# Encoder block on one core: order of the opening, products without use in front, low weights on GpSimd

## The chip, the cores and the metric

The kernel runs on one core of one Trainium2 chip, as one program. The metric is the device time of an execution in microseconds (us). Before the change it is 1885.11 us, the median of 3 runs (1883.92 to 1886.2).

## The reference, cut to what matters

One layer is applied to two groups of tokens, 2048 and 512 of them (five windows of 512), each with 16 meta tokens, at a width of 1024.

```python
u = rms_norm(h, norm_g)                    # h * rsqrt(mean(h*h) + eps) * g
qa, ka, va, za, qb, kb, vb, zb, ga, gb = jnp.split(u @ w_in, cuts, axis=-1)
o_a = neighbourhood_attention(qa, ka, va, na_rpb, n)
o_b = window_attention(qb, kb, vb, t5_bias, sink, n)
merged = sigmoid(ga) * ((o_a * silu(za)) @ w_proj_a) + sigmoid(gb) * ((o_b * silu(zb)) @ w_proj_b)
h = h + merged @ w_out                     # then a final rms_norm
```

Only the first part matters here: the norm and the projection of the last window (window 4) by 18 blocks of `w_in`, each 128 columns wide, and the passage to the next stage, which projects windows 0 and 1 together.

## The kernel before

**Split operands.** Every float32 operand of a product is kept as two tiles, a high one (the value rounded, made by ScalarE) and a low one (value minus high, made by VectorE or GpSimd). A product is three matmuls: high weight by high data (L146), high by low (L147), low weight by high data (L148). `split_part` (L206 to 208) does this for weights: L207 is the cast on ScalarE, L208 the subtraction on the engine that is passed in, else on VectorE in this stage. `split_w` (L210) does a weight block in two halves of 512 columns, so each block is two casts and two subtractions.

**The opening.** `start_w` fetches the first weight blocks, `prep_last` (L317) loads window 4 in four tiles `xt` of two row blocks each. For each row block `k` it makes the high operand on ScalarE (L334, a scaling by the norm's gain) and the low one on VectorE (L335). Then ScalarE squares the tile in place (L337) and VectorE adds the squares to `rs` (L339, L342). The row scale by the root of the mean square isn't applied to the operands but to the results, at eviction, so projections can start before the roots are known. After a first `yield`, `prep_last` sums `rs` over partitions with small matmuls (L360, L361), computes the roots on VectorE (`rsqrt`, L150 to 163, on five columns) and puts them on the diagonal of a tile (L177). After a second `yield` it spreads them over all partitions with matmuls (`spread`, L185) and copies them to `rs` (L370).

**The first stage.** `beside` (L933) runs the 18 projections one after the other. `alone` does one of them: it yields four times in a projection, and `beside` counts these yields in `q`. At `q` = 9 and `q` = 14 (the pair `own[1]`) it resumes `prep_last`. Until the second of these points the evictions are held back in a list (`held[1]`), since they need the roots; there it runs them. Before projection `i` the weights of projection `i + 1` are split and those of projection `i + 3` fetched. Weight buffers are double, so the cast of a block waits for the end of the projection before the last. `prep_first`, resumed at the counts in `at`, prepares windows 0 and 1 for the next stage in the meantime: squares (L418) and sums of squares (L420, L423: one window on VectorE, the other on GpSimd), roots, scalings (L377) and operand splits (L381 on ScalarE, L382 on VectorE). Its tiles of squares and the `xt` share one pool of four buffers (`ev`). Projections 0 to 7 make queries; 8 to 17 make keys and values, each in two parts of 256 and 272 columns.

**The passage.** After the last projection `sides_first` makes sums of weight blocks (L816 to L829) and splits them, and `begin` and `pairs` start the paired stage, whose products are all recorded at L850 (`product`).

**What sets the order.** TensorE's and SP's instructions stand in the order of the code. Those of ScalarE, VectorE and GpSimd are put in order by a scheduler when the program is built, from times that it assumes; on the chip each engine works its queue strictly in that order. Every DMA shown below is issued by SP through `move` (L142).

Of the kernel before, what the change touches and what calls it, by code (L numbers as in the profile page):

```python
# [9 lines left out]
F32 = mybir.dt.float32  # L10
F32R = mybir.dt.float32r
I32 = mybir.dt.int32
AF = mybir.ActivationFunctionType
# [4 lines left out]
P = 128  # L18
# [7 lines left out]
WTOK = 512  # L26
# [69 lines left out]
def encoder_block(ctx: ExitStack, tc: tile.TileContext, xT, x_end, w_in, w_pa, w_pb, w_o, norm_g, final_g,  # L96
                  final_row, bias_a0, bias_a1, bias_a2, bias_a3, bias_b, bias_b0, outT_p, outT_s, out_e):
    nc = tc.nc
# [29 lines left out]
    ones_r = const.tile([P, P], F32R, name="ones")  # L128
# [81 lines left out]
    def split_w(raw, engines=()):  # L210

        wt = wpool.tile([P, 2, KT * P], F32R, tag="wt", name="wt")
        for i, c in enumerate(range(0, KT * P, 4 * P)):
            split_part(wt[:, 0, c : c + 4 * P], wt[:, 1, c : c + 4 * P], raw[:, c : c + 4 * P], *engines[i : i + 1])
        return wt
# [94 lines left out]
    ps_t = ph.enter_context(tc.tile_pool(name="ps_t", bufs=3, space=PSUM))  # L310
# [6 lines left out]
    def prep_last(meta):  # L317


        w = NWIN - 1  # L320
        uh, ul = (operand(i, [P, KT, PITCH], f"u4{i}") for i in (5, 6))
        us[w] = (uh, ul, us[w][2] if w in us else uxp.tile([P, UW + N_META], F32, tag="rs4", name="rs4")[:, :UW])
        rs = us[w][2]
        for k in range(0, KT, 2):
            rows = xT[k * P : (k + 2) * P]
            xt = ev.tile([P, 2, WTOK], F32, tag="ev", name="xt")
            move(xt, rows[:, w * WTOK : (w + 1) * WTOK].rearrange("(k p) t -> p k t", p=P))
            if meta and k == 0:
                xm = st.tile([P, KT, N_META], F32, tag="xm", name="xm", bufs=1)
                move(xm, xT[:, TOK:].rearrange("(k p) t -> p k t", p=P))  # L330
            for j in range(2):
                g = ng[:, k + j : k + j + 1]
                h = uh[:, k + j, :WTOK]
                nc.scalar.mul(h, xt[:, j, :], g)  # L334
                nc.vector.scalar_tensor_tensor(ul[:, k + j, :WTOK], xt[:, j, :], g, f32(h), ALU.mult, ALU.subtract)  # L335
            if meta:
                nc.scalar.activation(xt, xt, AF.Square)  # L337
                if k == 0:
                    nc.vector.tensor_add(rs[:, :WTOK], xt[:, 0, :], xt[:, 1, :])  # L339
                else:  # L340
                    for j in range(2):
                        nc.vector.tensor_add(rs[:, :WTOK], rs[:, :WTOK], xt[:, j, :])  # L342
        if not meta:
            return
        t = ev.tile([P, WTOK], F32, tag="t", name="xms", bufs=3)
        a, b = (t[:, i * P : (i + 1) * P].rearrange("p (k m) -> p k m", m=N_META) for i in range(2))
        nc.vector.tensor_mul(a, xm, ng[:, :, None].broadcast_to([P, KT, N_META]))
        mh, ml = uh[:, :, WTOK:UW], ul[:, :, WTOK:UW]
        nc.scalar.copy(mh, a)
        nc.vector.tensor_sub(ml, a, f32(mh))  # L350
        nc.scalar.activation(b, xm, AF.Square)
        for n in (4, 2):
            nc.vector.tensor_add(b[:, :n], b[:, :n], b[:, n : 2 * n])
        nc.vector.tensor_add(rs[:, WTOK:], b[:, 0], b[:, 1])
        yield
        sq = st.tile([P, 32], F32, tag="sq", name="sq", bufs=1)[:, :5]
        nc.vector.memset(sq, 1.0)
        v = ps_t.tile([P, WTOK], F32, tag="vt", name="fin_v")
        for c in range(4):
            nc.tensor.matmul(v[:, c : c + 1], rs[:, c * P : (c + 1) * P], ones[:, 0:1], start=True, stop=True)  # L360
        nc.tensor.matmul(v[:N_META, 4:5], rs[:, WTOK:], ones[:, 0:1], start=True, stop=True)  # L361
        nc.scalar.copy(sq[:, :4], v[:, :4])
        nc.scalar.copy(sq[:N_META, 4:5], v[:N_META, 4:5])
        r = rsqrt(uxp, sq, P, 5)
        dgs = [ev.tile([P, WTOK], F32, tag="t", name="rs_dg", bufs=3) for _ in range(2)]
        diagonal(dgs[0], r[:, :4], P)
        diagonal(dgs[1], r[:N_META, 4:5], N_META)
        yield
        for dg, c0, m, nc_ in (dgs[0], 0, P, 4), (dgs[1], WTOK, N_META, 1):
            nc.scalar.copy(rs[:, c0 : c0 + nc_ * m], spread(ps_t, "vt", dg, m, nc_)[:, : nc_ * m])  # L370
        yield
# [561 lines left out]
    def beside(fs, raws, wts, own, wa, steps, at, zeros=iter(())):  # L933

        held = [own, None if own is None else []]
        ws = [*fs, *both[0]]
        lag[0] = 4
        mark[0] = None  # L940
        at = list(at)
        q = 0
        for i, f in enumerate(fs):
            if i:
                wts.append(split_w(raws[i + 1]))
                if i + 3 < len(ws):
                    raws.append(fetch_w(w_in[ws[i + 3]]))
                next(zeros, None)
            for _ in alone(f, wts[i], held):
                q += 1  # L950
                if own is not None and q in own[1]:
                    next(own[0])
                    if q == own[1][-1]:
                        for fn in held[1]:
                            fn()
                        held[1] = None
                while at and at[0] <= q:
                    at.pop(0)
                    next(steps)
                tick()  # L960
        for r in steps:
            if r == "last":
                break
        first = sides_first(raws[-2:], wts[-1])
        raw1 = fetch_w(w_in[both[1][0]])
        a = begin(both[0][0], wa, wts[-1], us[wa], ev)
        with tc.issue_after(copied[0]):
            for _ in steps:
                pass
        return a, first, raw1  # L970
# [8 lines left out]
    def start_w(fs):  # L979
        raws = [fetch_w(w_in[f]) for f in fs[:1]]  # L980
        wts = [split_w(raws[0])]
        yield raws, wts
        raws.append(fetch_w(w_in[fs[1]]))
        raws.append(fetch_w(w_in[fs[2]]))
        yield
        wts.append(split_w(raws[1]))
        raws.append(fetch_w(w_in[fs[3]]))
        yield

    def pass_(wa, a, first, raw1, ahead, extra, opening):  # L990
        with ExitStack() as pp:
            pool = [pp.enter_context(tc.tile_pool(name=f"p{i}", bufs=1, reuse_waits="tile")) for i in range(3)]
            return pairs(pool, wa, wa + 1, both, a, first.send(pool[2]), raw1, ahead, extra, opening)

    w0 = start_w(firsts)
    raws, wts = next(w0)
    own = prep_last(True)
    next(own)
    with tc.tile_pool(name="sp", bufs=1, reuse_waits="tile") as sp:
        loaded = []  # L1000
        steps = prep_first(sp, 0, loaded)
        next(w0)
        next(steps)
        next(w0)
        loaded.append(last_move[0])
        next(steps)
        zeros = zero_rows()
        next(zeros)
        begun = beside(firsts, raws, wts, (own, (9, 14)), 0, steps, [2, 20, 27, *(28 + 27 * i // 10 for i in range(16))],
                       zeros)  # L1010
    steps = [(0, 1), *((n, i) for n in range(1, KT) for i in (0, 1)), (KT, 0), (KT, 1), (KT, 2), (9, 1),
             *((j, i) for j in range(10, 18) for i in ((0, 2) if j % 2 == 0 else (1,)))]
# [680 lines left out]
```

## Time and profile before

| | before |
|---|---|
| median of 3 runs | 1885.11 us |
| the profiled execution | 1884.6 us |
| its span | 1882.6 us |
| TensorE (PE) busy | 1857.5 us, 99% |
| VectorE (DVE) busy | 1326.1 us, 70% |
| ScalarE (ACT) busy | 1144.5 us, 61% |
| GpSimd (POOL) busy | 729.2 us, 39% |
| TensorE's first product | 7.12 us |
| TensorE's first product of the paired stage | 122.38 us |

Times are in us from the start of the span. PE stands for TensorE, DVE for VectorE, ACT for ScalarE, POOL for GpSimd, SP for the engine that issues the DMAs. A row of a timeline gives the start, the time, the engine, the line of the code, the operation, what it writes and reads with shapes, and how many such instructions it merges; in brackets stands how long the engine had been idle, and what ended that. The time of a row covers an instruction's whole pipeline, so rows that follow each other overlap a little; from start to start a VectorE operation on 128 x 512 takes about 0.6 us where its row shows 0.68.

### The profile page before, as it was taken

The page shows a single profiled execution, that of the slowest core. Times are in us where ns is not written, and L with a number is a line of the kernel's source. Part 1 is how long each engine was busy: PE and PEld are TensorE (multiplying, and loading weights), DVE is VectorE, ACT ScalarE, POOL GpSimd, SP SyncE. Part 2 cuts the span into 40 slices and gives each one's busy share as a digit, 9 for nine tenths or more (in the row PEclk, how much of TensorE's full clock was granted, in tenths as well). Part 3 has the DMA queues.
Part 4 walks back from the last instruction along what each step waited for, and adds up shares of the span by engine and source line. Part 5 has one row for each costly group of instructions (what it writes and reads, how often), then busy time and mean ns, then how long its engine had stood idle before and what let it go on. Part 6 is the DMA issues. An engine that isn't in the chain of part 4 may idle for free. (4 is left out here: it accounts for less than half of the span.)

```text
span 1882.6 us, 29816 instructions
## 1 busy us (share of the span) xinstructions
PE 1857.5 (99%) x9797; PEld 1585.1 (84%) x9797; DVE 1326.1 (70%) x2961; ACT 1144.5 (61%) x2528; POOL 729.2 (39%) x558
## 2 busy tenths in 40 slices
PE   8999999999999999999999999999999999999998
PEld 6988888888888888888888888888888888888887
DVE  8985667556477565544457888878887877888874
ACT  6444444434365444444456797797789778878932
POOL 2005343323203222322324435656744763685420
PEclk9999999999999999999999999999999999999999
DMA  7675666655295677644259878977986997697483
GB/s 262 199 195 183 194 184 182 209 188 179 84 341 185 189 216 199 208 139 160 104 187 316 274 221 265 305 213 249 319 275 187 316 307 227 218 315 259 118 301 133
DMA packets 288145, 414.35 MB, mean 220 GB/s; under 512 B 117736, under 2 KB 162360, under 8 KB 286456
## 3 DMA queue, kind: packets, MB, share of 16 engines
q1 hardware_dynamic: 287704, 412.45, 68.1%
q8 instruction: 78, 1.28, 0.3%
q14 instruction: 75, 0.61, 0.1%
q10 hardware_dynamic: 288, 0.01, 0.0%
HBM read 303.46 MB, written 108.91 MB: 219 GB/s over the span
## 5 line engine op out<-in xcount | busy, mean ns | idle before, releaser
L208 POOL TENSOR_TENSOR wt<-wraw,wt 128x512 fp32r<-128x512 f32 x164 | 213.0, 1317 | 266.9 <-ACT wt L207 266.8
L850 PE MATMUL pa<-u,wt 128*128 128x512 f32 x1008 | 244.5, 392 | 2.1 <-ACT wt L207 1.1
L850 PE MATMUL pa<-u,x 128*128 128x512 f32 x984 | 236.7, 389 | 0.4 <-ACT u L861 0.4
L850 PEld LDWEIGHTS pa<-u,wt 128*128 128x128 f32 x1008 | 189.9, 189 | 42.4 <-ACT wt L207 1.5
L207 ACT CAST wt<-wraw 128x512 fp32r<-128x512 f32 x312 | 178.0, 619 | 74.8 <-PE mm L148 29.8
L850 PEld LDWEIGHTS pa<-u,x 128*128 128x128 f32 x984 | 184.5, 188 | 39.2 <-ACT u L861 0.8
L821 POOL TENSOR_TENSOR s<-wraw,raw 128x512 f32<-128x512 f32 x40 | 58.2, 1456 | 279.4 <-DVE x L208 279.4
L146 PE MATMUL mm<-u,wt 128*128 128x512 f32 (+2 forms) x416 | 150.4, 362 | 7.1 <-ACT u L334 7.1
L816 POOL TENSOR_TENSOR s<-raw 128x512 f32<-128x512 f32 x40 | 58.1, 1454 | 232.8 <-DMA raw<-in_w_in_dram 116.0
L147 PE MATMUL mm<-u,wt 128*128 128x512 f32 (+2 forms) x416 | 146.8, 353 | 1.1 <-DVE u L335 1.1
L148 PE MATMUL mm<-u,wt 128*128 128x512 f32 (+2 forms) x416 | 146.6, 352 | 0.0
L208 DVE TENSOR_TENSOR wt<-wraw,wt 128x512 fp32r<-128x512 f32 x148 | 104.5, 744 | 52.3 <-ACT wt L207 52.1
L850 PE MATMUL pe<-u,wt 128*128 128x512 f32 x504 | 121.4, 390 | 0.0
L850 PE MATMUL pc<-u,wt 128*128 128x512 f32 x504 | 121.1, 389 | 0.0
L850 PE MATMUL pe<-u,x 128*128 128x512 f32 x480 | 115.3, 389 | 0.0
L850 PEld LDWEIGHTS pe<-u,wt 128*128 128x128 f32 x504 | 94.6, 188 | 19.6
L850 PEld LDWEIGHTS pc<-u,wt 128*128 128x128 f32 x504 | 94.6, 188 | 19.6
L1145 DVE TENSOR_TENSOR pl<-tp,ph 128x384 fp32r<-128x384 f32 (+6 forms) x160 | 94.9, 593 | 20.9 <-ACT ph L1144 18.7
L1144 ACT CAST ph<-tp 128x384 fp32r<-128x384 f32 (+6 forms) x160 | 81.5, 510 | 43.0 <-PE tp L1141 41.4
L146 PE MATMUL pso<-mh,wt 128*128 128x512 f32 x256 | 107.1, 418 | 0.0
L829 POOL TENSOR_TENSOR s<-wraw,s 128x512 f32<-128x512 f32 x40 | 54.0, 1350 | 136.3 <-DVE wt L208 136.3
L850 PEld LDWEIGHTS pe<-u,x 128*128 128x128 f32 x480 | 90.1, 188 | 18.7
(258 smaller groups left out, 5024.8 us busy)
## 6 DMA issues: line engine op xcount, KB each, us to landing
wraw<-in_w_in_dram SPq DMA_DIRECT2D x86, 512.0 KB
raw<-in_w_in_dram SPq DMA_DIRECT2D x40, 512.0 KB
q<-qa SPq DMA_DIRECT2D x40, 512.0 KB
wraw<-in_w_o_dram SPq DMA_DIRECT2D x32, 512.0 KB
kbt<-kb SPq DMA_DIRECT2D x32, 384.0 KB
qa<-evq SPq DMA_DIRECT2D x20, 512.0 KB
qb<-evq SPq DMA_DIRECT2D x20, 512.0 KB
ka<-evk SPq DMA_DIRECT2D x20, 512.0 KB
```

Source lines behind the costliest of these rows:

```text
L146: nc.tensor.matmul(ps, wh, uh, start=first, stop=False)
L147: nc.tensor.matmul(ps, wh, ul, start=False, stop=False)
L148: nc.tensor.matmul(ps, wl, uh, start=False, stop=last)
L207: nc.scalar.copy(h, r)
L208: low[0] = (eng or lo_eng[0]).tensor_sub(l, r, f32(h)).ins
L816: eng.tensor_add(s1, a21, a22)
L821: eng.tensor_sub(s3, a11, a21)
L829: eng.tensor_sub(s4, a12, s2)
L850: nc.tensor.matmul(ps, wt[:, a, s], u[:, b, kk, :], start=first and kk == 0 and i == 0, stop=kk == 3 and i == 2, skip_group_check=True)
L1144: nc.scalar.copy(ph_[:kb, a], tb)
L1145: nc.vector.tensor_sub(pl_[:kb, a], tb, f32(ph_[:kb, a]))
```

## The change

Four things are changed.

1. In `prep_last` the squares come after all scalings in the code. Their sums are made by two engines: GpSimd adds the squares of the first two tiles, VectorE those of the last two, and VectorE adds the two sums.
2. Ahead of everything TensorE multiplies a tile of ones by itself 22 times, into a bank that nobody reads.
3. In `beside`, for the 18 projections of window 4, low weights go to GpSimd: the second half of the blocks split at `i` = 2 and 3, both halves from `i` = 4 on.
4. `prep_last` is resumed for the spread at `q` = 16 instead of 14, the end of the fourth projection instead of its middle.

Nothing else is edited, but the scheduler puts ScalarE's, VectorE's and GpSimd's instructions into another order up to about 140 us.

```diff
+        xts = []
         for k in range(0, KT, 2):
...
-            if meta:
-                nc.scalar.activation(xt, xt, AF.Square)
-                if k == 0:
-                    nc.vector.tensor_add(rs[:, :WTOK], xt[:, 0, :], xt[:, 1, :])
-                else:
-                    for j in range(2):
-                        nc.vector.tensor_add(rs[:, :WTOK], rs[:, :WTOK], xt[:, j, :])
+            xts.append(xt)
         if not meta:
             return
+        for xt in xts:
+            nc.scalar.activation(xt, xt, AF.Square)
+        parts = xts[0][:, 0, :], rs[:, :WTOK]
+        for sums_, first, eng in (parts[0], xts[0][:, 0, :], nc.gpsimd), (parts[1], xts[2][:, 0, :], nc.vector):
+            n = 0 if eng is nc.gpsimd else 2
+            eng.tensor_add(sums_, first, xts[n][:, 1, :])
+            for j in range(2):
+                eng.tensor_add(sums_, sums_, xts[n + 1][:, j, :])
+        nc.vector.tensor_add(parts[1], parts[1], parts[0])
...
-                wts.append(split_w(raws[i + 1]))
+                wts.append(split_w(raws[i + 1], (nc.vector if i < 4 else nc.gpsimd, nc.gpsimd) if own is not None and i > 1
+                                   else ()))
...
+    idle = ps_t.tile([P, WTOK], F32, tag="vt", name="idle")
+    for _ in range(22):
+        nc.tensor.matmul(idle[:, :P], ones_r, ones_r, start=True, stop=True)
...
-        begun = beside(firsts, raws, wts, (own, (9, 14)), 0, steps, [2, 20, 27, *(28 + 27 * i // 10 for i in range(16))],
+        begun = beside(firsts, raws, wts, (own, (9, 16)), 0, steps, [2, 20, 27, *(28 + 27 * i // 10 for i in range(16))],
```

On VectorE in the opening, from the third low operand on (`u` is the operand of window 4, `rs` its sum of squares, `wt<-wraw` a low weight), the rows before are:

```order
L335 SCALAR_TENSOR_TENSOR u_293<-xt,ng,u_292 128x512
L354 TENSOR_TENSOR rs_294<-xms 128x16
L335 SCALAR_TENSOR_TENSOR u_293<-xt,ng,u_292 128x512
L339 TENSOR_TENSOR rs_294<-xt 128x512
L335 SCALAR_TENSOR_TENSOR u_293<-xt,ng,u_292 128x512 x2
L342 TENSOR_TENSOR rs_294<-rs_294,xt 128x512
L335 SCALAR_TENSOR_TENSOR u_293<-xt,ng,u_292 128x512
L342 TENSOR_TENSOR rs_294<-rs_294,xt 128x512
L335 SCALAR_TENSOR_TENSOR u_293<-xt,ng,u_292 128x512
```

and now (lines below the edit are numbered 1 to 8 higher):

```order
L336 SCALAR_TENSOR_TENSOR u_316<-xt,ng,u_315 128x512
L358 TENSOR_TENSOR rs_317<-xms 128x16
L336 SCALAR_TENSOR_TENSOR u_316<-xt,ng,u_315 128x512 x5
L208 TENSOR_TENSOR wt<-wraw,wt 128x512 x2
L345 TENSOR_TENSOR rs_317<-xt 128x512
```

The three adds between the low operands are gone; GpSimd has three adds of `xt` in front of its queue instead. ScalarE's queue of the opening is the same in both programs, squares of the first two tiles between the scalings.

On GpSimd, after those three adds, the sums of squares of `prep_first` (`rsp`) were followed by the paired stage's first sum of weights:

```order
L420 TENSOR_TENSOR rsp_349<-sq 128x512
L423 TENSOR_TENSOR rsp_349<-rsp_349,sq 128x512 x6
```

and now the low weights stand between and behind them:

```order
L424 TENSOR_TENSOR rsp_372<-sq 128x512
L427 TENSOR_TENSOR rsp_372<-rsp_372,sq 128x512 x2
L208 TENSOR_TENSOR wt<-wraw,wt 128x512
L427 TENSOR_TENSOR rsp_372<-rsp_372,sq 128x512 x4
L208 TENSOR_TENSOR wt<-wraw,wt 128x512 x29
```

Thirty halves of low weights have moved to GpSimd's queue; VectorE's has lost as many.

On ScalarE at the passage to the paired stage (`wt<-s` are casts of sums of weights, `s<-pa` a copy of a bank, `u<-x` parts of the last operands) stood:

```order
L207 CAST wt<-s 128x512
L861 COPY s_1640<-pa 128x512
L381 CAST u_1661<-x_352 128x512 x4
L381 CAST u_1670<-x_353 128x512
L207 CAST wt<-s 128x512
L381 CAST u_1670<-x_353 128x512 x3
```

and now:

```order
L207 CAST wt<-s 128x512 x2
L865 COPY s_1663<-pa 128x512
L385 CAST u_1684<-x_375 128x512 x4
L385 CAST u_1693<-x_376 128x512 x4
```

The second cast of a weight sum has moved ahead of the copy and of all operand parts. On VectorE the two low halves of these sums have likewise moved ahead of all of them (the second stood behind five), and the first of the sums ahead of the last projection's last eviction.

## The prediction

> **What bounds the kernel now.** I read the page first, then the windows of 20 us, then TensorE's waits and the timelines of single engines.
>
> ```profile
> span 1882.6 us, 29816 instructions
> PE 1857.5 (99%) x9797; PEld 1585.1 (84%) x9797; DVE 1326.1 (70%) x2961; ACT 1144.5 (61%) x2528; POOL 729.2 (39%) x558
> ```
>
> TensorE is busy for 99%, so only its holes can be won, or new ones made. The program's rows differ from those of before only up to about 140 us, so these windows matter:
>
> ```profile
> 0.00:20.00 20.00, 12.59 (x43) 9.40 (x44) 14.84 (x30) 16.00 (x24) 1.97 (x7) 1.00 0.93 329
> 20.00:40.00 20.00, 18.98 (x93) 15.62 (x92) 19.04 (x32) 11.32 (x18) 8.47 (x7) 1.00 0.57 202
> 120.00:140.00 20.00, 17.93 (x83) 14.40 (x82) 15.07 (x29) 10.32 (x20) 1.18 (x1) 0.91 0.77 234
> ```
>
> After the window's length come the busy times of PE, PEld, DVE, ACT and POOL, the granted clock and DMA. Holes are before 20 us, one between 20 and 40, and one after 120, with the clock at 0.91. TensorE's waits up to 150 us, and its timeline, name them:
>
> ```profile
> PE pa L850 <- ACT wt L207: 1.1, 1, 1.1
> PE rs_rb L185 <- DVE rs_dg L177: 1.0, 1, 1.0
> PE pa L850 <- DVE wt L208: 1.0, 1, 1.0
> ...
> 7.12 0.79 PE L146 MATMUL mm<-u,wt 128*128 128x512 f32 x1 [7.12 <-ACT u L334]
> 11.89 0.39 PE L147 MATMUL mm<-u,wt 128*128 128x512 f32 x1
> 15.21 0.50 PE L147 MATMUL mm<-u,wt 128*128 128x512 f32 x1 [0.30 <-DVE u L335]
> 15.78 0.39 PE L146 MATMUL mm<-u,wt 128*128 128x512 f32 x1
> 31.72 1.48 PE L185 MATMUL rs_rb<-rs_dg,ones 128*128 128x128 f32 x10 [1.02 <-DVE rs_dg L177]
> ```
>
> A product takes 0.79 us at first and 0.39 from 11.89; the first projection ends at 15.78, its last piece late because VectorE's low half of it was late.
>
> **Idle products: 0.** They raise the clock before 7.12. That would be worth some 2.5 us (ten products in the 4.8 us from 7.12 to 11.89, against 0.23 each at full clock, twelve in 2.76 in the rows of the transition below) if operands were there. They are not: TensorE had caught up by 15.21 and waited. The first projection's end is set by VectorE, next.
>
> **Squares added by two engines: +1.4.** VectorE and ScalarE in the opening:
>
> ```profile
> 10.35 0.69 DVE L339 TENSOR_TENSOR rs<-xt 128x512 f32<-128x512 f32 x1
> 10.96 1.42 DVE L335 SCALAR_TENSOR_TENSOR u<-xt,ng,u 128x512 fp32r<-128x512 f32 x2
> 12.53 0.69 DVE L342 TENSOR_TENSOR rs<-rs,xt 128x512 f32<-128x512 f32 x1
> 13.14 0.75 DVE L335 SCALAR_TENSOR_TENSOR u<-xt,ng,u 128x512 fp32r<-128x512 f32 x1
> 13.81 0.68 DVE L342 TENSOR_TENSOR rs<-rs,xt 128x512 f32<-128x512 f32 x1
> 14.41 0.74 DVE L335 SCALAR_TENSOR_TENSOR u<-xt,ng,u 128x512 fp32r<-128x512 f32 x1
> ...
> 9.28 1.04 ACT L337 ACTIVATE xt<-xt 128x1024 f32<-128x1024 f32 x1
> 10.23 1.32 ACT L334 ACTIVATE u<-xt,ng 128x512 fp32r<-128x512 f32 x2
> 11.45 1.04 ACT L337 ACTIVATE xt<-xt 128x1024 f32<-128x1024 f32 x1
> 12.40 1.32 ACT L334 ACTIVATE u<-xt,ng 128x512 fp32r<-128x512 f32 x2
> ```
>
> ScalarE's queue keeps its order: two squares still stand ahead of the last two pairs of scalings, so the eighth low half can't start before about 13.8 (12.40 + 1.32, and the seventh's 0.75 from 13.14). Without the add at 13.81 it would run at 13.8 instead of 14.41: a gain of 0.6 to 0.7, if GpSimd's three adds cost nothing. What they cost VectorE is seen where both engines run:
>
> ```profile
> 25.69 5.43 POOL L423 TENSOR_TENSOR rsp<-rsp,sq 128x512 f32<-128x512 f32 x4 [2.26 <-ACT sq L418]
> ...
> 27.04 0.17 DVE L162 TENSOR_TENSOR rs<-rs,rs 128x5 f32<-128x5 f32 x1
> 27.24 1.15 DVE L163 SCALAR_TENSOR_TENSOR rs<-rs,rs 128x5 f32<-128x5 f32 x1
> ...
> 141.43 1.75 POOL L821 TENSOR_TENSOR s<-wraw,raw 128x512 f32<-128x512 f32 x1
> ...
> 141.95 0.68 DVE L281 TENSOR_TENSOR tq<-pe,u 128x512 f32<-128x512 f32 x1
> ```
>
> An operation on five columns, normally 0.17, takes 1.15 beside GpSimd's adds (1.36 each). One that reads PSUM passes in its usual 0.68. So a GpSimd add holds up a VectorE operation with two SBUF inputs for 1.15, and when both queues are full they alternate. The Trainium skill says the same, and it speaks against this change (SBUF — State Buffer, "Who interferes with whom"): a VectorE instruction with two SBUF inputs contends with a GpSimd one that reads SBUF, and the second to issue waits for the whole of the first. The trace agrees, 1.15 against 0.17.
>
> Applied to the opening: the first add starts at 10.4 (after the square from 9.28) and ends its hold at 11.6; low halves five and six run to 13.0; the second add holds to 14.15; the seventh runs to 14.8; the third add holds to 15.95; the eighth ends at 16.6. The first projection then ends at 17.15 instead of 15.78: +1.4, with -0.7 as the other end.
>
> **Roots spread later: -1.0.** The spread moves from half of the fourth projection to its end, 12 products or 2.7 us later. The roots come some 1.5 to 2 us later (the sums start 1.4 later, and one low weight is put ahead of them), so the wait of 1.02 goes; all of it returns if they are over 3.7 us late (2.7 + 1.02). Evictions start later with it, and so do stores on SP and the weight fetch queued behind them (L142); that is in the next term.
>
> **GpSimd makes low weights: +1.6.** The stretch from 51 to 122.5 us by engine, then L281 and L208 alone:
>
> ```profile
> 51.00:122.50 71.50, 71.50 (x556) 69.91 (x555) 66.23 (x131) 34.26 (x68) 0.00 (x0) 1.00 0.62 182
> ...
> 51.00:122.50 71.50, 10.65 (x23) 1.00 0.62 182
> ...
> 51.00:122.50 71.50, 15.59 (x24) 0.00 (x0) 1.00 0.62 182
> ```
>
> VectorE loses 24 low weights, 14.4 us at 0.6 from start to start, and keeps 51.8. GpSimd gains 24 that hold it up for 1.15 each: 27.6. GpSimd is then busy for about 24 x 1.3 = 31 of 71.5 us (44%), so that share of L281's 10.65, which reads PSUM, passes beside it: 4.6. Sum: 51.8 + 27.6 - 4.6 = 74.8 in 71.5. VectorE ends 3.3 us late. Of this TensorE feels between nothing (operands of the next stage are done early) and all (ScalarE's casts stand in one queue behind values that VectorE makes); I take the middle, 1.6. Where it shows first:
>
> ```profile
> 59.05 0.62 ACT L207 CAST wt<-wraw 128x512 fp32r<-128x512 f32 x1 [3.26 <-DMA wraw<-in_w_in_dram]
> 61.43 0.28 PE L146 MATMUL mm<-u,wt 128*128 128x256 f32 x1
> ```
>
> This cast ends 1.8 us ahead of its projection, and a low half now takes 1.3 instead of 0.6. A fetch 1 us later already stalls, and this one will be late: it stands in SP's queue (L142) behind the stores of the first evictions, which now start after the later spread. SP waits longer there too: a fetch into a buffer needs the low half that read it, now GpSimd's, some 2 us after the cast instead of 1.2. Behind such a fetch stand only stores of q, k and v, which nobody reads in this stretch, and the next fetch, two projections (some 11 us) ahead of its use. The evictions are held back half a projection longer, with four of five PSUM banks in use; the fifth projection takes the fifth, so TensorE doesn't wait for that.
>
> **Transition: -4.2.** The first products of the paired stage:
>
> ```profile
> 122.38 2.92 PE L850 MATMUL pa<-u,wt 128*128 128x512 f32 x12
> 125.14 2.88 PE L850 MATMUL pc<-u,wt 128*128 128x512 f32 x12
> 129.09 0.73 PE L850 MATMUL pa<-u,wt 128*128 128x512 f32 x2 [1.07 <-ACT wt L207]
> 130.82 4.14 PE L850 MATMUL pa<-u,wt 128*128 128x512 f32 x10 [1.00 <-DVE wt L208]
> 134.81 2.91 PE L850 MATMUL pe<-u,wt 128*128 128x512 f32 x12
> ...
> 128.42 0.62 ACT L207 CAST wt<-s 128x512 fp32r<-128x512 f32 x1
> ...
> 130.09 0.68 DVE L208 TENSOR_TENSOR wt<-s,wt 128x512 fp32r<-128x512 f32 x1
> ```
>
> Twelve take 2.76, so pe should start at 122.38 + 3 x 2.76 = 130.66; it starts at 134.81, 4.15 late: two waits and then products at 0.4 each. ScalarE cast the operand at 128.42, behind five others, and VectorE made its low half at 130.09. In the new order both casts stand ahead of those five and both low halves ahead of all operand parts. VectorE needs some 3.2 us from the last eviction to the first of them (three sums, evictions, one low half), so even 3 us late it has it near 129 against 127.9. I take -4.2; the other end is 0, if VectorE comes over 4 us late and the clock falls again.
>
> **Sum.** 0 + 1.4 - 1.0 + 1.6 - 4.2 = -2.2 us. The profiled run took 1884.6 (span 1882.6), 0.5 under the median of 1885.11. Median forecast: 1882.9.
>
> **Rivals.** *Nothing is lost to contention*: VectorE's late work has slack everywhere, operand low halves slip past GpSimd's adds: -0.7 - 1.0 + 0 - 4.2 = -5.9, 1879.2. For it: operands of the next stage are finished early. Against: the 1.15 rows. 0.27.
>
> *VectorE and GpSimd together become the bound* (slower): no PSUM read lies beside a GpSimd operation and TensorE feels all: 51.8 + 27.6 - 71.5 = +7.9, held at weight after weight from 61 us on. 1.4 - 1.0 + 7.9 - 4.2 = +4.1, 1889.2. It ends slower by over 0.2% once this term passes 7.6. For it: the stretch has only 5.3 us of VectorE idle. 0.18.
>
> *The clock falls in the opening* (a cost on top of the forecast): at full clock the first projection waits about 1.1 us three times, and the rows at 129.09 and 130.82 show two such waits followed by ten products in 4.14. That adds some 1.8: -0.4, 1884.7. The Trainium skill (TensorE: Matmul & The Clock Gate, "What's actually happening") has the clock fall only after an idle window of about 3.4 us; by that nothing is added. The trace shows the fall after waits of 1.07 and 1.00 with two products between, so I keep a chance: 0.13.
>
> **How the numbers follow.** The forecast has 0.42. Runs of this kernel can tell about 0.2% (3.8 us: 1881.3 to 1888.9) from no change. An eighth of the forecast's chance lies below 1881.3: faster 0.27 + 0.05 = 0.32; slower 0.18; the same 0.37 + 0.13 = 0.50. The range takes in the first rival nearly whole and reaches to the second: 1878.5 to 1889.2.
>
> **What would show it.** Idle products right: full clock at 7 us, first projection's end unmoved by them. Adds right: VectorE's fifth to eighth low halves 1 us and more each. Roots right: no wait at L185. Low weights right: GpSimd operations at 1.3 to 1.75, VectorE near full from 51 us, waits at L146 or L148 for GpSimd's weights. Transition right: both casts before 125 us and no wait at L850. Wrong is the forecast if the first projection ends before 15.5, if TensorE stalls over 4 us between 55 and 122, or if the waits at L850 stay.

## The result, and the profile after

The change makes the kernel slower: 1895.01 us (median of 6 runs, 1892.29 to 1897.69) against 1884.64 for the kernel before (6 runs), a ratio of 1.0052 with a 95% interval of 1.0039 to 1.0065. The profiled execution took 1892.8 us, 8.2 more than the one of before.

The profile's first lines, then the windows of 20 us and the stretch of the low weights, as for before:

```profile
span 1891.0 us, 29886 instructions
PE 1864.6 (99%) x9819; PEld 1588.7 (84%) x9819; DVE 1329.7 (70%) x2928; ACT 1144.2 (61%) x2528; POOL 780.3 (41%) x591
```

```profile
20.00:40.00 20.00, 20.00 (x98) 16.33 (x97) 19.38 (x25) 10.51 (x17) 15.97 (x11) 1.00 0.64 219
60.00:80.00 20.00, 18.03 (x134) 16.85 (x134) 19.07 (x26) 8.49 (x16) 9.33 (x6) 1.00 0.54 187
80.00:100.00 20.00, 18.08 (x143) 17.46 (x143) 19.96 (x31) 8.73 (x18) 10.95 (x6) 1.00 0.52 168
120.00:140.00 20.00, 16.95 (x108) 14.77 (x107) 16.15 (x29) 9.54 (x21) 6.73 (x4) 1.00 0.69 178
51.00:131.00 80.00, 74.47 (x560) 70.84 (x559) 69.86 (x107) 34.36 (x67) 38.25 (x24) 1.00 0.54 162
```

The hole between 20 and 40 us is gone. New ones of 2 us each stand in 60 to 80 and 80 to 100. The last row is the stretch of before's row from 51 to 122.5, now 80 us long because the paired stage starts at 130.87 instead of 122.38. TensorE's waits up to 170 us (total, times, longest) name the new holes:

```profile
PE mm L148 <- POOL wt L208: 3.0, 2, 1.9
PE vt L642 <- DVE vn L254: 1.6, 1, 1.6
PE idle L1002 <- DVE ones L129: 1.6, 1, 1.6
PE pa L854 <- ACT s L865: 1.1, 1, 1.1
PE mm L146 <- ACT wt L207: 0.9, 1, 0.9
...
PE pa L854 <- DVE wt L208: 0.3, 1, 0.3
```

How far the changed kernel is behind, from the starts of the same projections in the two timelines:

| | before | after | behind |
|---|---|---|---|
| second projection | 15.78 | 17.09 | 1.31 |
| fifth | 36.00 | 36.01 | 0.01 |
| ninth | 61.43 | 63.37 | 1.94 |
| tenth | 67.31 | 70.95 | 3.64 |
| thirteenth | 84.93 | 90.74 | 5.81 |
| seventeenth | 109.99 | 116.65 | 6.66 |
| paired stage | 122.38 | 130.87 | 8.49 |
| its product pe | 134.81 | 141.02 | 6.21 |

At the fifth projection the changed kernel has made good what it lost in the opening; all that follows is new. Most steps up are a wait or two. The first and the second of the large ones in four queues (SP's fetch, ScalarE's cast, GpSimd's low halves, TensorE's products):

```profile
58.03 0.32 SPq L142 DMA_DIRECT2D qb<-evq  x1
58.45 0.38 SPq L142 DMA_DIRECT2D wraw<-in_w_in_dram  x1
```

```profile
62.70 1.14 ACT L207 CAST wt<-wraw 128x512 fp32r<-128x512 f32 x2 [2.23 <-DMA wraw<-in_w_in_dram]
80.63 0.62 ACT L385 CAST u<-tt 128x512 fp32r<-128x512 f32 x1 [1.96 <-DVE tt L449]
81.16 1.13 ACT L207 CAST wt<-wraw 128x512 fp32r<-128x512 f32 x2
```

```profile
63.39 3.21 POOL L208 TENSOR_TENSOR wt<-wraw,wt 128x512 fp32r<-128x512 f32 x2 [5.94 <-ACT wt L207]
81.85 4.33 POOL L208 TENSOR_TENSOR wt<-wraw,wt 128x512 fp32r<-128x512 f32 x2 [4.87 <-ACT wt L207]
```

```profile
63.37 0.38 PE L146 MATMUL mm<-u,wt 128*128 128x256 f32 x1 [0.88 <-ACT wt L207]
64.96 0.38 PE L148 MATMUL mm<-u,wt 128*128 128x256 f32 x1 [1.09 <-POOL wt L208]
85.00 0.39 PE L148 MATMUL mm<-u,wt 128*128 128x256 f32 x1 [1.90 <-POOL wt L208]
```

The fetch left SP 4.2 us later than before (54.23), behind a store of values that VectorE made late. So the cast came 3.65 us later than before's 59.05, and two halves that had taken VectorE 0.69 us each took GpSimd 3.21. At 81 us no fetch is late: ScalarE's cast stands in its queue behind a value that VectorE made late (`tt`, a wait of 1.96), and the two low halves take 4.33.

Groups of GpSimd and of VectorE from 51 to 131 us (count, busy time, mean ns of one):

```profile
L208 POOL TENSOR_TENSOR wt<-wraw,wt 128x512 fp32r<-128x512 f32 x24 | 38.2, 1615 | 43.9 <-ACT wt L207 43.9
```

```profile
L386 DVE TENSOR_TENSOR u<-x,u 128x512 fp32r<-128x512 f32 x12 | 14.8, 1229 | 0.0
L281 DVE TENSOR_TENSOR tkv<-mm,rs 128x256 f32<-128x256 f32 x18 | 7.2, 407 | 0.0
L465 DVE TENSOR_TENSOR x<-x,tt 128x512 f32<-128x512 f32 x4 | 6.7, 1681 | 0.1
```

The first of VectorE's lines as it was before, from 51 to 122.5 us:

```profile
L382 DVE TENSOR_TENSOR u<-x,u 128x512 fp32r<-128x512 f32 x12 | 8.0, 682 | 0.0
```

Low halves of operands, 682 ns before, take 1229; L281, which reads PSUM, is as short as before (416 then).

### The profile page after: what moved, and what is told of

The parts are those of the page before. It is cut to its first block, busy times and chain, and to the rows that moved or that the text cites. A ratio compares the mean times of both kernels' runs of the same rounds, so it can differ in the third digit from the quotient of the medians.

```text
span 1891.0 us, 29886 instructions
## 1 busy us (share of the span) xinstructions
PE 1864.6 (99%) x9819; PEld 1588.7 (84%) x9819; DVE 1329.7 (70%) x2928; ACT 1144.2 (61%) x2528; POOL 780.3 (41%) x591
## 4 chain that ended last, share of the span: by engine, by line
PE 80%; DVE 6%; DMA 6%; ACT 4%; issue 2%; SPq 1%; POOL 1%; ACTq 0%; DVEq 0%
PE pa L854 23%; PE pe L854 11%; PE pc L854 6%; PE tp L1149 3%; PE mm L147 2%; PE mm L148 2%; PE mm L146 2%; PE pso L148 2%; PE pso L146 2%; PE pso L147 2%; DMA sgb<-gb 2%; PE psa L146 2%; PE psa L148 2%; PE psa L147 2%; PE tp L1251 2%
## 5 line engine op out<-in xcount | busy, mean ns | idle before, releaser
L208 POOL TENSOR_TENSOR wt<-wraw,wt 128x512 fp32r<-128x512 f32 x194 | 260.0, 1358 | 317.7 <-ACT wt L207 317.5
L207 ACT CAST wt<-wraw 128x512 fp32r<-128x512 f32 x312 | 177.8, 619 | 55.0 <-DMA wraw<-in_w_in_dram 19.2
L208 DVE TENSOR_TENSOR wt<-wraw,wt 128x512 fp32r<-128x512 f32 x118 | 87.3, 777 | 47.2 <-ACT wt L207 47.0
L1062 ACT ACTIVATE s<-s,nm 128x384 f32<-128x384 f32 (+5 forms) x160 | 87.1, 544 | 30.9 <-DVE nm L1055 29.9
```

The costliest lines, as they stand in the source:

```text
L207: nc.scalar.copy(h, r)
L208: low[0] = (eng or lo_eng[0]).tensor_sub(l, r, f32(h)).ins
L1062: nc.scalar.activation(out, s, AF.Exp, bias=nm, scale=-1.0, accum_out=sm)
```

## Experiments

Twelve more programs ran, one of them the kernel before itself. Each ratio is against the kernel before, run beside it. "Paired stage" is its first product in the profile, "pe" the product that started 12.43 us behind it before.

| run | ratio | 95% interval | paired stage | to pe |
|---|---|---|---|---|
| before | | | 122.38 | 12.43 |
| before, profiled again | | | 123.72 | 12.26 |
| after | 1.0052 | 1.0039 to 1.0065 | 130.87 | 10.15 |
| e1_low_on_vector | 1.0017 | 1.0008 to 1.0027 | 123.36 | 13.63 |
| e2_low_alone | 1.0049 | 1.0031 to 1.0067 | 130.73 | 10.36 |
| e3_unused_adds | 1.0071 | 1.0055 to 1.0086 | 134.67 | 12.84 |
| e4_one_half | 1.0007 | 0.9997 to 1.0017 | 125.88 | 9.18 |
| e5_idle_alone | 1.0003 | 0.9992 to 1.0014 | 122.15 | 12.41 |
| e6_squares_alone | 1.0022 | 1.0014 to 1.0031 | 123.81 | 14.08 |
| e7_spread_alone | 1.0004 | 0.9996 to 1.0013 | 121.42 | 12.30 |
| e8_late_halves | 0.9981 | 0.9972 to 0.9989 | 121.93 | 9.52 |
| e10_wide_idle | 1.0006 | 0.9997 to 1.0015 | 122.98 | 10.87 |
| e11_two_halves | 0.9981 | 0.9972 to 0.9990 | 121.55 | 8.19 |
| e12_unused_zeros | 1.0009 | 0.9999 to 1.0019 | 124.82 | 10.85 |

### The changed kernel with low weights on VectorE again

```diff
-                wts.append(split_w(raws[i + 1], (nc.vector if i < 4 else nc.gpsimd, nc.gpsimd) if own is not None and i > 1
-                                   else ()))
+                wts.append(split_w(raws[i + 1]))
```

> The changed kernel with all low weights of the first stage back on VectorE; squares, idle products and the later spread stay. Three theories. Port: GpSimd's subtractions hold up VectorE by some 1.15 us each, VectorE comes late, and weights and casts behind it: then the loss goes, about 1885 us (1883 to 1887), no waits for weights from 55 to 122 us. Late weight: a low weight takes 1.3 us on GpSimd instead of 0.6 and delays the fetch behind it, and VectorE's being held has no part in it: 1885 us too. Late spread: the evictions moved to the end of the fourth projection make stores and fetches late, GpSimd is not the cause: 1892 us or more, with the waits at 62 to 85 us still there.

Measured: 1888.75 us, and the paired stage at 123.36, 7.5 us earlier than in the changed kernel. TensorE's waits at the passage:

```profile
PE pa L854 <- ACT wt L207: 2.1, 1, 2.1
...
PE pa L854 <- DVE wt L208: 1.2, 1, 1.2
```

So the loss up to 131 us hangs on GpSimd's low weights, and the better passage too: without them the scheduler puts the second cast behind the copy and seven operand parts again. SP's late fetch leaves at 56.92 here, and no wait over 0.2 us follows: of the 4.2 us by which it is late in the changed kernel, 2.7 come from the other three parts and are covered by slack, and 1.5 come from GpSimd's low weights. The other three parts together still cost 0.08% to 0.27%.

### The kernel before with GpSimd's low weights alone

```diff
-                wts.append(split_w(raws[i + 1]))
+                wts.append(split_w(raws[i + 1], (nc.vector if i < 4 else nc.gpsimd, nc.gpsimd) if own is not None and i > 1
+                                   else ()))
```

> The kernel before with low weights on GpSimd as the only change. Port and late weight: 1889 to 1895 us, waits for GpSimd's low weights between 60 and 125 us. Late spread: 1881 to 1885 us, since the evictions stand where they did.

Measured: 1894.38, a loss as large as the changed kernel's from this part alone; the paired stage starts at 130.73 with the spread where it was. So the loss doesn't need the later spread. It is made up otherwise, though: 3.0 us stand ahead of the fifth projection (38.98 against 36.00), where TensorE waits 2.4 us for the roots and the granted clock is then 0.87 from 36 to 44 us. Later come a wait of 1.9 for a low weight and one of 1.1 for `vn`, as at 85 and 125 us in the changed kernel; the two waits at 63 us don't occur, so these need the change's other parts as well.

### Subtractions on GpSimd that nobody waits for

VectorE keeps every low weight. GpSimd subtracts 384 columns twice per block into columns that nobody reads.

```diff
                 wts.append(split_w(raws[i + 1]))
+                for n in range(0 if own is None or i < 2 else 2):
+                    h = f32(wts[-1][:, 0, n * 4 * P : n * 4 * P + 384]).rearrange("p (k c) -> p k c", k=KT)
+                    nc.gpsimd.tensor_sub(us[NWIN - 1][n % 2][:, :, UW:PITCH], h, h)
```

> The kernel before, with two subtractions on GpSimd beside each weight block from the third on (128 x 384, read from the block's high half, written to columns that nobody reads), 32 in all; VectorE still makes every low weight, and no fetch or product waits for GpSimd. Port: VectorE has 66.2 us of work between 51 and 122.5 us and is held up for 24 x 0.9 = 21.6 more, less some 3 beside PSUM reads: 85 in 71.5 us, so 8 to 14 us slower, 1893 to 1899 us. Late weight: no weight comes from GpSimd, so 1884 to 1886 us. Late spread: the same 1884 to 1886 us.

Measured: 1898.34, more than the change itself. TensorE now waits for VectorE's low weights, and VectorE is all but full:

```profile
PE mm L148 <- DVE wt L208: 3.9, 4, 2.1
PE rs_rb L185 <- DVE rs_dg L177: 3.3, 1, 3.3
PE pa L850 <- DVE wt L208: 1.6, 1, 1.6
```

```profile
51.00:134.50 83.50, 79.64 (x578) 75.86 (x577) 79.04 (x143) 35.15 (x68) 29.11 (x24) 0.98 0.56 168
```

Nobody waits for these subtractions, so what GpSimd holds up on VectorE is enough for a loss of this size; 5.5 of the 12.3 us stand ahead of the fifth projection (41.48 against 36.00), where the roots come late. That GpSimd's slow delivery adds nothing in the changed kernel isn't shown: no run has slow delivery without the hold.

### Half as many low weights on GpSimd

The edit is made in the changed kernel.

```diff
-                wts.append(split_w(raws[i + 1], (nc.vector if i < 4 else nc.gpsimd, nc.gpsimd) if own is not None and i > 1
-                                   else ()))
+                wts.append(split_w(raws[i + 1], (nc.vector, nc.gpsimd) if own is not None and i > 1 else ()))
```

> The changed kernel with the second half of each low weight on GpSimd and the first on VectorE (16 halves instead of 30). Port: 51.8 + 7.2 + 13.8 - 2.3 = 70.5 us of VectorE's time in 71.5, so nearly nothing is late: 1882 to 1887 us. Late weight: the second half is needed 1.4 us after the first, so waits shrink but fetches stay late: 1885 to 1889 us. Late spread: 1892 us or more.

Measured: 1886.11, no difference clear of noise. With one half of a block on each engine TensorE waits for nothing between 56 and 130 us. Of the 3.5 us by which the paired stage is late, 3.1 stand between 36 and 52 us: a wait of 0.9 at L432 for VectorE's sums of squares, three of which take 3.18 us beside a low weight on GpSimd, and a granted clock of 0.50 from 46 to 48 us after it. The passage gains 3.25 (9.18 against 12.43).

### Idle products alone

```diff
+    idle = ps_t.tile([P, WTOK], F32, tag="vt", name="idle")
+    for _ in range(22):
+        nc.tensor.matmul(idle[:, :P], ones_r, ones_r, start=True, stop=True)
     w0 = start_w(firsts)
```

> The kernel before with the 22 idle products alone. No other instruction moves. 'They neither help nor cost': the first products still take 0.79 us each until about 12 us, the first projection ends within 0.2 us of 15.78, the time is within 0.2% of before (1881 to 1889). Rival, 'they raise the clock, and what hid it in the changed kernel were its late operands': the first products take 0.39 to 0.6 from 7.12 on; TensorE waits more at the high-by-low products instead; the end of the first projection moves by less than 0.3 us, or comes up to 0.5 earlier, and the time is again within 0.2%. The length of the products before 12 us tells them apart, not the time.

Measured: 1885.92, the same. TensorE's opening:

```profile
1.62 4.96 PE L997 MATMUL idle<-ones 128*128 128x128 f32 x22 [1.62 <-DVE ones L129]
7.25 0.80 PE L146 MATMUL mm<-u,wt 128*128 128x512 f32 x1 [0.67 <-ACT u L334]
8.04 0.79 PE L147 MATMUL mm<-u,wt 128*128 128x512 f32 x1
8.63 0.63 PE L148 MATMUL mm<-u,wt 128*128 128x512 f32 x1
...
11.48 0.40 PE L146 MATMUL mm<-u,wt 128*128 128x512 f32 x1
...
15.28 0.51 PE L147 MATMUL mm<-u,wt 128*128 128x512 f32 x1 [0.29 <-DVE u L335]
15.62 0.40 PE L148 MATMUL mm<-u,wt 128*128 128x512 f32 x1
15.85 0.40 PE L146 MATMUL mm<-u,wt 128*128 128x512 f32 x1
```

They did not raise the clock: the first product still takes 0.80, as in the three other profiles with these products (0.79 to 0.80), and 0.4 is reached at 11.48. Without any idle products it was reached at 11.89 (before), about 11.1 (the later spread alone) and 13.2 (the version with eight halves), so this start varies by 2 us by itself. The first projection ends where it did, with VectorE's last low half.

### Squares by two engines alone

The edit is the change's whole part in `prep_last`; the rest is as before.

```diff
-                nc.scalar.activation(xt, xt, AF.Square)
...
+        for xt in xts:
+            nc.scalar.activation(xt, xt, AF.Square)
+        parts = xts[0][:, 0, :], rs[:, :WTOK]
...
```

> The kernel before with the squares' part alone: squares behind the scalings in the code, their sums by GpSimd and VectorE. Port theory (a GpSimd add holds each VectorE operation with two SBUF inputs): VectorE's fifth to eighth low halves take 1 us and more each, the second projection starts near 17.1 instead of 15.78 (+1.3); the roots come later against a spread that has not moved, so a wait of 2 to 3 us stands at the spread. Rival, 'the adds cost nothing, the opening of the changed kernel is late through another of its parts': second projection starts at 15.1 to 15.8. Time: before + 1 to + 4 us with the first, 0 to -1 with the second.

Measured: 1889.67, slower by 0.14% to 0.31%. The second projection starts at 17.14, and the wait for the roots is 1.1, not the 2 to 3 expected. The paired stage is 1.43 us late, the term as predicted; the passage is worse by another 2 us (1.65 of it up to pe; waits of 2.1 and 0.9, and a granted clock of 0.83 from 120 to 140 us).

### The later spread alone

```diff
-        begun = beside(firsts, raws, wts, (own, (9, 14)), 0, steps, [2, 20, 27, *(28 + 27 * i // 10 for i in range(16))],
+        begun = beside(firsts, raws, wts, (own, (9, 16)), 0, steps, [2, 20, 27, *(28 + 27 * i // 10 for i in range(16))],
```

> The kernel before with the roots' spread at the end of the fourth projection alone. Theory 1, 'the spread is worth its wait': the wait of 1.02 us at L185 goes, nothing else moves up to 120 us, and the end comes 1 us earlier plus or minus the transition's order: within 0.2% of before. Theory 2, 'the later evictions cost': VectorE's evictions and the stores behind them start 2.7 us later, a cast near 62 us comes late by over 1.8 us and TensorE stalls there by 1 to 3 us: +0 to +2 us. In the changed kernel no such stall could be told from GpSimd's hold.

Measured: 1885.53, the same. The wait at L185 is gone, and the paired stage starts 0.96 earlier (121.42). No cast is late enough to stall a projection, so the later evictions cost nothing without GpSimd's hold.

### Second halves late in the stage only

The kernel before with the later spread of the run above, and:

```diff
-                wts.append(split_w(raws[i + 1]))
+                wts.append(split_w(raws[i + 1], (nc.vector, nc.gpsimd) if own is not None and i > 9 else ()))
```

> The kernel before with the later spread and the second low half of the blocks split at i = 10 and later on GpSimd (8 halves), no GpSimd squares and no idle products. If what the change gains is the spread's 1.0 us and the transition's 3 to 4 us, and what it loses is GpSimd's hold in the opening and over 24 halves, this version keeps the gain and pays for 8 holds of 0.55 to 1.15 (4 to 9 us of VectorE's work, in a stretch where it had 5 us idle, and later in the stretch than before): first product of the paired stage at 121.4 to 123, pe at 130.2 to 132, time 1879 to 1882, faster by 0.2 to 0.3%. Rival, 'any GpSimd low weights cost what they bring': 1884 to 1887, VectorE late at the transition and waits at the paired stage's first products again.

Measured: 1881.90, faster by 0.11% to 0.28%. The passage gains 2.9, and the stage ahead of it loses 0.5 of the spread's 1.0. VectorE is as busy as before from 51 to 122.5 us (66.46 of 71.5): eight holds took what eight low weights freed.

### The kernel before once more

> The kernel before, unchanged, profiled once more, for one question: the profile of before waits only 0.8 us in all for VectorE between 1340 and 1360 us, and five other programs, whose instructions there are the same, wait 2.5 to 3.9. 'It varies from execution to execution' (DMA engines are full there, and a fetch lands earlier or later): this profile waits anything from 0.8 to 4 us there, likelier 2 to 4, with a span of 1884 to 1886 when it does. 'An effect of the changes': it waits 0.8 again, within 0.3.

The question came from aligning the profiles: up to about 1336 us the changed kernel is 6.3 us behind, after 1376 it is 8.9. There the DMA engines are full in all programs, and VectorE waits for a fetch (`sgb`), TensorE for VectorE: 0.8 us in the profile of before, 3.1 in that of after. The unchanged kernel, profiled again, waits 2.2 there (span 1882.7, as before; the 1884 to 1886 expected with that did not come):

```profile
PE tp L1141 <- DVE pr L1065: 2.2, 2, 1.3
```

So about half of the 2.6 us, at least, is what one execution differs from another by: the unchanged kernel falls 1.4 us further behind its first profile in this stretch, and makes up 2.0 by 1600 us. The change's own part of the profile's difference can't be told more closely than some 6 to 8 us.

### Idle products of 512 columns

```diff
+    idle = ps_t.tile([P, WTOK], F32, tag="vt", name="idle")
+    for _ in range(10):
+        nc.tensor.matmul(idle, ones_r, ones_r[:, None, :].broadcast_to([P, 4, P]), start=True, stop=True)
     w0 = start_w(firsts)
```

> The kernel before with 10 idle products of 512 columns instead of 22 of 128: they stream without pause, where those of 128 columns stood 0.225 us apart, twice what a 512-column product at the same clock takes for each 128 columns. 'The clock follows how much TensorE streams': at 512 columns the clock rises while they run or soon after, the first products take 0.39 to 0.5 instead of 0.79 and 0.63, all is at 0.39 before 9.5 us. Rival, 'what comes ahead of the first real product does not count': 0.79 and 0.63 again until 11 to 13 us. In both cases the end of the first projection stays within 0.3 us of 15.8, since VectorE's last low half ends there, and the time within 0.2% of before (1881 to 1889).

Measured: 1885.36, the same. The opening has both halves of the answer:

```profile
1.63 3.87 PE L997 MATMUL idle<-ones 128*128 128x512 f32 x10 [1.63 <-DVE ones L129]
7.07 0.51 PE L146 MATMUL mm<-u,wt 128*128 128x512 f32 x1 [1.57 <-ACT u L334]
8.49 0.79 PE L147 MATMUL mm<-u,wt 128*128 128x512 f32 x1 [0.92 <-DVE u L335]
9.08 0.63 PE L148 MATMUL mm<-u,wt 128*128 128x512 f32 x1
...
14.63 0.43 PE L146 MATMUL mm<-u,wt 128*128 128x512 f32 x1
...
16.75 0.39 PE L146 MATMUL mm<-u,wt 128*128 128x512 f32 x1
```

Products that stream did raise the clock, in this one profile: the first real one takes 0.51. Then come pauses of 1.57 and 0.92 us (the second for a meta tile's load, 0.7 us later in this execution), and the clock is low again until 14.6. The second projection starts at 16.75, 1.0 later than before and with no wait ahead of it: a miss for the expectation of 0.3. The Trainium skill (TensorE: Matmul & The Clock Gate, "What's actually happening") says that the clock is released after a busy window of about 3.4 us and falls after an idle one, and that the windows run on regardless of when a kernel starts. The 3.87 us of streaming and the start that varies by 2 us agree; the 4.96 us of narrow products agree only if products 0.225 us apart don't count as busy, which no run here shows; the fall after two pauses of 1.57 and 0.92 with one product between comes sooner than that page's idle window.

### Fewer halves still

The later spread, and `i > 14` in the line of the version above. The expectation speaks of two halves; in the trace GpSimd makes three.

```diff
-                wts.append(split_w(raws[i + 1]))
+                wts.append(split_w(raws[i + 1], (nc.vector, nc.gpsimd) if own is not None and i > 14 else ()))
```

> The kernel before with the later spread and only two low halves on GpSimd, the second ones of the last two blocks. Theory, 'the gain at the passage comes from the order of the queues, which already turns with two halves, and every further half only holds VectorE up': the waits of 2.1 us at the paired stage's first products go, pe starts 3.5 to 5.2 us earlier than before (1.0 of it the spread), and the time is 1880 to 1882, faster by 0.15 to 0.3%, not slower than the version with eight halves. Rival, 'the gain came from VectorE being relieved of eight halves': with two it is late again at the first products, a wait of 1 to 2 us stays there, and the time is 1883 to 1885.

Measured: 1879.88 against 1883.61, faster by 0.10% to 0.28%, the same as with eight. TensorE's passage:

```profile
121.55 2.92 PE L850 MATMUL pa<-u,wt 128*128 128x512 f32 x12
124.30 2.88 PE L850 MATMUL pc<-u,wt 128*128 128x512 f32 x12
127.02 2.88 PE L850 MATMUL pa<-u,wt 128*128 128x512 f32 x12
129.74 2.88 PE L850 MATMUL pe<-u,wt 128*128 128x512 f32 x12
```

No wait is left, and pe stands 8.19 us behind the first product instead of 12.43: 4.24 gained. VectorE is relieved of only three halves and is as busy as before (66.43 us from 51 to 122.5, 66.23 before), so the order of the queues brings it: both casts of weight sums stand ahead of the copy (123.78 and 124.91). Some of it is the clock, 1.00 from 120 to 140 us instead of 0.91.

### GpSimd writes that read next to nothing

```diff
                 wts.append(split_w(raws[i + 1]))
+                for n in range(0 if own is None or i < 2 else 2):
+                    pad = f32(us[NWIN - 1][n][:, :, UW:PITCH])
+                    nc.gpsimd.tensor_copy(us[NWIN - 1][n][:, 0, UW : UW + 1], f32(wts[-1][:, 0, n * 4 * P : n * 4 * P + 1]))
+                    for _ in range(4):
+                        nc.gpsimd.memset(pad, 0.0)
```

> The kernel before, and for each block split from i = 2 on GpSimd does work that nobody waits for and that reads next to nothing: one element per row copied from the high weight (so that it starts when the unused subtractions of the other run did), then four times zeros into 128x384 unread columns, about 0.35 us each (0.3 for 96x256 in the profile of before), twice per block: 28 x 4 writes, some 39 us of GpSimd from 40 to 120 us, where the unused subtractions took 34. VectorE keeps every low weight. 'What holds VectorE up is GpSimd reading SBUF': VectorE's operations with two SBUF inputs keep their 0.68 us, the first product of the paired stage stands within 1.5 us of 122.4, the time is 1881 to 1889. Rival, 'any GpSimd work on SBUF holds VectorE up': VectorE's means rise to 1.0 and more, the paired stage begins 5 to 12 us later, the time is 1891 to 1899 as with the unused subtractions.

Measured: 1885.51, the same. GpSimd is busier than ever, and VectorE doesn't notice (window, then VectorE's group of low weights):

```profile
51.00:122.50 71.50, 71.50 (x548) 69.48 (x547) 65.50 (x128) 34.41 (x68) 56.81 (x116) 1.00 0.60 176
```

```profile
L208 DVE TENSOR_TENSOR wt<-wraw,wt 128x512 fp32r<-128x512 f32 x24 | 15.6, 686 | 0.5 <-ACT wt L207 0.4
```

The paired stage is 2.4 us late, past the 1.5 expected, but all of it stands between 36 and 52 us. GpSimd's sums of squares, which do read SBUF, queue among these writes and end at 34.2 us instead of 31.1; VectorE's own sums come late beside them, TensorE waits 1.1 us for these at L428, and the granted clock is 0.50 from 44 to 46 us after that wait. VectorE's and ScalarE's instructions up to the paired stage stand in the same order as before, here and with the unused subtractions, so no other order of the queues is behind the difference. So what holds VectorE up is GpSimd reading SBUF, not its being busy or writing. This is what the Trainium skill's page SBUF — State Buffer ("Who interferes with whom") says: two SBUF inputs contend with a GpSimd instruction that reads SBUF, not with one that only writes it. The runs agree, 686 ns beside 56.81 us of writes, and 1229 for a like operation beside 38.2 us of low weights.

## Why the prediction was wrong

The forecast was 1882.9 and no measurable change; it came out 1895.0, beyond the range.

**The step that failed: GpSimd's low weights, "+1.6".** The forecast had VectorE at 74.8 us of work in 71.5 and let TensorE feel the middle of nothing and 3.3; TensorE felt 8.5. The work was sized about right, even too high: the same 107 operations took 69.86 us against 50.6 before (66.23 less 15.59 of low weights), a hold of 19.2 us for 24 low weights, 0.80 each, where 23.0 was forecast (27.6 less 4.6). What failed is the rule from that to TensorE. I took VectorE's lateness at the end of the stretch as the bound. By that rule the measured work, 69.86 in 71.5, would have cost nothing, yet TensorE fell 8.5 us behind between the fifth projection (36.01 after, 36.00 before) and the paired stage.

It felt five single waits: 0.3 for sums of squares, 0.9 and 1.1 at 63 us, 1.9 at 85, 1.6 at 125, together 5.8; some 2.7 more lie around these waits and in the thirteenth projection, which takes 6.42 instead of 5.87, and aren't named by any row. The three at 63 and 85 us stand at the end of a chain of queues: VectorE's late value holds a store on SP or a cast on ScalarE, behind which the next weight's fetch or cast stands, and a GpSimd pair of 3.2 to 4.3 us comes on top of that. The other two are waits for VectorE itself, the one at 125 us behind two operations that take 1.78 and 1.76 us beside a GpSimd pair, and 0.74 and 0.68 alone. A queue has no average slack. The row that I had quoted (a cast 1.8 us ahead of its projection) pointed to the place, and I priced it away.

The term also left out what lies ahead of its stretch. Six of the 30 halves are made before 51 us, and VectorE's first evictions start at 42.05, against 39.34 with the low weights back on VectorE. And a stretch's total hides where VectorE is full: it is so from 80 to 100 us (19.96 of 20), but works only 2.83 of the 8 us from 52 to 60. Being full isn't enough either: before, VectorE is busy for 39.47 of the 40 us from 60 to 100, and no product waits there.

The slower rival had the size, +7.9 against 8.5, but not the reason: over the stretch GpSimd is busy for 38.25 of 80 us and VectorE for 69.86, and L281 passes beside GpSimd (407 ns, 416 before). That its number fits is luck.

**The transition, "-4.2".** Right as a price, not here: 4.24 when VectorE and SP are on time (three halves), 3.25 with half the low weights, 2.28 in the changed kernel, so 1.9 of the miss stands here. Both casts did move ahead, but the fetch of the block that is summed stood on SP behind late stores. VectorE's first sum and ScalarE's first cast, after:

```profile
134.45 0.69 DVE L820 TENSOR_TENSOR s<-wraw 128x512 f32<-128x512 f32 x1 [1.48 <-DMA wraw<-in_w_in_dram]
```

```profile
135.25 0.62 ACT L207 CAST wt<-s 128x512 fp32r<-128x512 f32 x1 [2.92 <-DVE s L820]
```

The cast comes 4.38 us after the paired stage's first product, with three halves 2.23 (123.78 against 121.55).

**Squares by two engines, "+1.4".** Right: VectorE's last two low halves took 3.16 us beside two GpSimd adds, and the second projection started at 17.09, forecast 17.15.

```profile
12.81 3.11 POOL L347 TENSOR_TENSOR xt<-xt 128x512 f32<-128x512 f32 x2 [0.96 <-ACT xt L341]
```

```profile
13.31 3.16 DVE L336 SCALAR_TENSOR_TENSOR u<-xt,ng,u 128x512 fp32r<-128x512 f32 x2 [0.24 <-ACT u L335]
```

**Roots later, "-1.0".** Right: 0.96 alone, and no wait at L185 after.

**Idle products, "0".** Right in the sum, wrong in the reason: I had the clock at full speed by 7 us. The first product still takes 0.79 in the changed kernel, and where wide products did raise the clock, the pauses after them let it fall again.

**The sum.** By the measured sizes up to pe: the squares' 1.3 is made good by the later spread, so that nothing is lost at the fifth projection; 8.5 for the low weights and 2.3 less at the passage make 6.2, and the table has 6.21. The profile ends 8.4 behind, most of the rest from the stretch at 1340 us that varies. The medians are further apart (0.39% to 0.65%, some 7 to 12 us); the profiled execution of the changed kernel was 2.2 us below its median, and where these 2 us lie stays open. That the parts alone add up to more (0.49, 0.22, 0.04 and 0.03%, in all 0.78%) than the whole is likely because the low weights alone make the roots late for the early spread (3.0 us at the fifth projection), which the later spread covers, and because the squares' worse passage doesn't occur with the other order; no run shows these pairs alone.

## What to carry to other kernels

Moving work to an idle engine is priced by what it holds up, not by its own time: here each GpSimd subtraction that reads SBUF cost VectorE 0.80 us to save it 0.65. Where engines feed each other through queues in fixed order, compare the latency of single items with their slack, weight by weight; a stretch's total says neither where an engine is full nor which late value is waited for. A large edit can hold a small useful part: three low halves and a later point for the spread bring 0.2%, most of it because they turn the order of two casts.

## What was not expected of the hardware

- Twenty-two 128-column products in 4.96 us did not raise TensorE's clock, in four profiles; ten of 512 columns in 3.87 us did, in one (the first real product 0.51 instead of 0.80), and two pauses of 1.57 and 0.92 us with one product between undid it.
- At the passage the same two waits of 1.1 and 1.0 us do not always lower the clock: from 120 to 140 us it is 0.91 in both profiles of the kernel before and 1.00 with the wide idle products, which change nothing there. With the same waits pe then starts 10.87 behind the paired stage's first product instead of 12.43, so some 1.6 of the 4.2 that the passage costs is the clock, by estimate.
- A wait in front of narrow products can lower it too: after waits of 0.9 and 1.1 us for sums of squares, followed by the 16 one-column products of L432 and L428, the granted clock was 0.50 for some 2 us (half the low weights on GpSimd; GpSimd writes), and the sixth projection took 7.16 and 6.91 us instead of 5.58. After a wait of 0.3 in the changed kernel it stayed at 1.00.
- GpSimd writing to SBUF for 56.81 of 71.50 us left VectorE's operations at 686 ns.
